# First block: 24 reciprocal square roots worked out on GpSimd instead of VectorE

## The chip, the cores and the metric

One core of a Trainium2 chip runs the whole program in one launch. The metric is the device time of an execution in microseconds (us). Engines are named as the profile names them: PE (TensorE matrix products; PEld are its weight loads), DVE (VectorE), ACT (ScalarE), POOL (GpSimd) and SP (SyncE, which issues the weight transfers). Each takes its instructions in a fixed order.

## The reference, cut to what matters

Two blocks follow each other. The first has two layers over 256 tokens `x` and 256 context tokens `xc`; the second has two layers of another kind (feed-forward, mixer, feed-forward). Only the first block's norms are touched.

```python
def _rmsnorm(x, g):
    y = xf * lax.rsqrt(jnp.mean(xf * xf, axis=-1, keepdims=True) + RMS_EPS)
    return y * g
def _layernorm(x, g, b):
    y = (xf - mu) * lax.rsqrt(var + LN_EPS)
    return y * g + b
...
def _layer(x, xc, ...):
    h = _rmsnorm(x, norm_g) * (1 + scale) + shift            # modulate()
    hp = h @ w_in
    q, k, v: _rmsnorm(hp[Q]) @ w_uq, _rmsnorm(hp[KV]) @ w_ukv  # mla()
    conv: silu(_layernorm(depthwise_conv31(glu))) @ w_pw      # conv_out()
    sgu:  u * (w_s @ _layernorm(v))                           # sgu()
    y = concat(attn, conv, fourier, sgu) * silu(hp[GATE])
    x = x + gate * (y @ w_out)
```

## The kernel before

Four tiles of 128 tokens (t = 0, 1 of `x`, t = 2, 3 of `xc`) go through the first layer together; in the second layer the context tiles only give keys and values. All of a layer's weights stream through as tiles of 512 KB: DMA (`raw`), ACT rounds them (`whi`), DVE takes the rest (`wlo`), and PE makes three products of each (`u` for the input projection, `yo` for the output projection). Beside this stream, Python generators give the side work of each branch: `mla` (queries, keys, values), `sgu`, `conv` (31 steps of `acc` on DVE) and `conv_out`, `fourier`, `attend`, and `ada_rest` (long dot products `adaj` on DVE, which make the modulation vectors of the next stages). `modulate` makes the second layer's input.

A planner in the kernel (`Sched`) keeps a clock for each engine. `S.dve`, `S.act` and `S.pool` add a planned cost and issue the instruction; a generator is resumed when the planned clock passes what it waits for. The framework's own list scheduler then settles each engine's final order from these instructions and their dependencies. So planned lengths decide who stands behind whom, on all engines, and on the chip each engine waits in that order.

The norms need 1/sqrt(w) for one or two numbers in each row. `rsqrt` does it by a bit trick (`rs_y` from the integer view of `w`, `rs_h` = -w/2) and three Newton steps, each instruction dependent on the one before. On DVE a step for one column is two instructions (`rs_t`, `rs_y`). There are 24 such chains in the first block: 12 in `layernorm` (six from `sgu`, six from `conv_out`; ten DVE instructions from `rwl` to `lnb`), 4 in `modulate` (nine), and 8 in `mla` (six with two columns, twelve instructions; two with one, nine). A `layernorm` chain's result goes to ACT (`ln`), for `sgu` then to two DVE instructions (`ln<-ln,rows`) and the PE product `sgum`; for `conv_out` to PE transposes (`tpc<-ident,ln`), ACT (`cs`) and the PE product `pw`. A `modulate` chain scales `xn`, which PE transposes (`tpx`) for the next layer's `u` and `kv`. An `mla` chain's result is the scale of ACT's copies `qkf` and `V`.

Before the change POOL only clears buffers (MEMSET of `qkf`, `qz`, `glu`) and issues a few transfers (`xc`, `final_g`, `grow`).

Of the kernel before, what the change touches and what calls it, by code (L numbers as in the profile page):

```python
# [19 lines left out]
EPS = 1e-6  # L20
# [73 lines left out]
LN_EPS = 1e-5  # L94
# [72 lines left out]
class Sched:  # L167
# [201 lines left out]

def rsqrt(S, ch, pool, w, n, tag):

    y = pool.tile([P, n], F32, tag=tag + "y", name="rs_y", bufs=4)
    h = pool.tile([P, n], F32, tag=tag + "h", name="rs_h")
    t = pool.tile([P, n], F32, tag=tag + "t", name="rs_t")
    S.dve(ch, n, "tensor_scalar", y.bitcast(I32), w.bitcast(I32), -0.5, float(0x5F3759DF), op0=ALU.mult, op1=ALU.add)
    S.dve(ch, n, "tensor_scalar", h, w, -0.5, None, op0=ALU.mult)
    for _ in range(3):
        if n == 1:  # L380
            S.dve(ch, n, "scalar_tensor_tensor", t, y, h, y, op0=ALU.mult, op1=ALU.mult, x=0.06)
        else:
            S.dve(ch, n, "tensor_tensor", t, y, y, op=ALU.mult)
            S.dve(ch, n, "tensor_tensor", t, t, h, op=ALU.mult)
        S.dve(ch, n, "scalar_tensor_tensor", y, t, 1.5, y, op0=ALU.add, op1=ALU.mult)
    return y


# [577 lines left out]
class First:  # L966
# [293 lines left out]
    def modulate(self, t, l, x, ch, ss, ev):  # L1260

        S, s = self.S, t // 2
        new = self.hp.tile if t < 2 else self.p1.tile
        kw = (dict(tag="hhi"), dict(tag="hlo")) if t < 2 else (dict(tag="s4", bufs=S4),) * 2
        hi, lo = (new([P, KT, P], F32R, name=n, **k) for n, k in zip(("hhi", "hlo"), kw))
        w = self.small.tile([P, 1], F32, tag="rw", name="rw")
        S.dve(ch, 1, "scalar_tensor_tensor", w, ss[:, 0:1], EPS, ss[:, 1:2], op0=ALU.add, op1=ALU.add)
        r = rsqrt(S, ch, self.small, w, 1, "r")
        xn = [self.normed(Chain(ch.t), x, r, n, n == 1) for n in range(2)]
        yield ch  # L1270
        for n in range(2):
# [12 lines left out]
            S.act(ch, 512, "copy", hi[:, h, :], f)
            S.dve(ch, 512, "tensor_sub", lo[:, h, :], f, hi[:, h, :].bitcast(F32))
            if n == 0:
                S.done(ev, ch)
        self.hs[t] = lambda k: (hi[:, k, :], lo[:, k, :])


    def layernorm(self, ch, src, n):

        S = self.S
        st = self.small.tile([P, 6], F32, tag="bn", name="bn")
        mv = self.small.tile([P, 2], F32, tag="mv", name="mv", bufs=4)
        S.dve(ch, n, "bn_stats", st, src)
        S.dve(ch, 6, "bn_aggr", mv, st)
        w = self.small.tile([P, 1], F32, tag="rw", name="rwl")
        S.dve(ch, 1, "tensor_scalar", w, mv[:, 1:2], LN_EPS, None, op0=ALU.add)
        r = rsqrt(S, ch, self.small, w, 1, "r")  # L1300
        b = self.small.tile([P, 1], F32, tag="lnb", name="lnb", bufs=4)
        S.dve(ch, 1, "scalar_tensor_tensor", b, mv[:, 0:1], -1.0, r, op0=ALU.mult, op1=ALU.mult)
        z = self.w2([P, 256], "ln")
        S.act(ch, 256, "activation", z, src, AF.Identity, scale=r, bias=b, x=0.15)
        return z
# [216 lines left out]
    def mla(self, t, ps, kv_only=False):  # L1522
        nc, S, l = self.nc, self.S, self.l[t]
        s, i = divmod(t, 2)
        o = 0 if kv_only else 256
        kv0 = 96 if kv_only else 256
        ch = S.chain()
        w = 160 if kv_only else 416
        p0 = 96 if kv_only else 0
        a = self.w2([P, 416], "mla")  # L1530
        S.act(ch, w, "copy", a[:, :w], ps[:, p0:p0 + w])
        ss = self.small.tile([P, 2], F32, tag="ssm", name="ssm", bufs=4)
        if not kv_only:

            jk = self.w2([P, 256], "jq")
            S.act(ch, 256, "activation", jk, a[:, :256], AF.Square, scale=math.sqrt(96.0 / 256), accum_out=ss[:, 0:1], x=0.09)
        jk = self.w2([P, 256], "jk")
        S.act(ch, 128, "activation", jk[:, :P], a[:, o:o + P], AF.Square, scale=math.sqrt(1.0 / 128), accum_out=ss[:, 1:2],
              x=0.09)
        if kv_only:  # L1540
            S.dve(ch, 1, "tensor_scalar", ss[:, 1:2], ss[:, 1:2], EPS, None, op0=ALU.add)
            r = rk = rsqrt(S, ch, self.small, ss[:, 1:2], 1, "r")
        else:
            S.dve(ch, 2, "tensor_tensor", ss, ss, self.eps2, op=ALU.add)
            r = rsqrt(S, ch, self.small, ss, 2, "r2")
# [24 lines left out]
        S.act(ck, 256, "mul", self.L[l].V[t], pv[:, :, 64:], rk, x=0.09)  # L1570
        kr = a[:, o + P:o + P + 32]
        if s == 0:
            self.rotate(ck, kv[:, :, 64:96], kr.unsqueeze(1).to_broadcast([P, 4, 32]), i)
        else:
            S.act(ck, 128, "copy", kv[:, :, 64:96], kr.unsqueeze(1).to_broadcast([P, 4, 32]))
        cq = None
        if not kv_only:
            qv = kf[:, :, 1, :]
            pq = self.psum("ps", "pq")
            cq = S.chain()  # L1580
            for c in range(2):
# [364 lines left out]
```

## Time and profile before

| what | value |
|---|---|
| median of 3 runs | 1449.67 us (1449.08 to 1450.29) |
| the profiled execution, its own time | 1447.77 us |
| its span in the profile | 1446.0 us (1.77 us lie around it) |
| PE busy | 1403.1 us (97%) |
| DVE busy | 1002.7 us (69%) |
| ACT busy | 765.8 us (53%) |
| POOL busy | 30.0 us (2%), 46 instructions |
| TensorE clock granted, mean | 0.996 |

The first block takes the first 430 us or so of the span. A busy PE is not PE at its peak, since records of products overlap; what PE waits for is read from the timeline's brackets. The shares over the whole span hide that DVE is busy for nearly all of some stretches of the first block.

### The profile page before, as it was taken

How to read it: one execution, taken by the hardware profiler on the slowest of the kernel's cores; microseconds unless marked ns; L12 is line 12 of the kernel's file. 1: busy time of each engine (PE TensorE's matmuls, PEld its weight loads, DVE VectorE, ACT ScalarE, POOL GpSimd, SP SyncE). 2: the span in 40 equal slices, each digit the busy share in tenths (PEclk: the TensorE clock that was granted, in tenths of full speed). 3: DMA queues.
4: the chain of work that ended last, by engine and by line, in shares of the span. 5: the costliest groups of instructions: out<-in, count | busy, mean ns of one | idle time of the engine just before them, and what ended most of it. 6: DMA issues, size and time to landing. Idle time of an engine off the chain costs nothing.

```text
span 1446.0 us, 19092 instructions
## 1 busy us (share of the span) xinstructions
PE 1403.1 (97%) x6766; PEld 1134.5 (78%) x6766; DVE 1002.7 (69%) x2175; ACT 765.8 (53%) x1348; POOL 30.0 (2%) x46
## 2 busy tenths in 40 slices
PE   7999997999999999999999999999999999999997
PEld 4778886777877888777878888788887778788886
DVE  4899978779787555587886555765555878865554
ACT  4465533576565444567655444554445676554442
POOL 1000000000000000000000000000000000000000
PEclk9999999999999999999999999999999999999999
DMA  8751455333456555653446566566566534466551
GB/s 304 238 172 59 128 192 162 123 124 121 159 189 209 186 188 188 190 186 121 139 139 204 189 180 186 173 193 187 188 189 189 182 125 134 143 200 186 185 186 58
DMA packets 69088, 245.64 MB, mean 170 GB/s; under 512 B 7841, under 2 KB 8097, under 8 KB 68865
## 3 DMA queue, kind: packets, MB, share of 16 engines
q1 hardware_dynamic: 66384, 235.11, 51.1%
q0 software_dynamic: 2176, 8.79, 1.8%
q8 instruction: 53, 0.87, 0.2%
q10 hardware_dynamic: 432, 0.53, 0.1%
q14 instruction: 43, 0.34, 0.1%
HBM read 243.35 MB, written 1.05 MB: 169 GB/s over the span
## 4 chain that ended last, share of the span: by engine, by line
PE 79%; DVE 11%; DMA 4%; ACT 3%; issue 2%; SPq 0%; DVEq 0%; ACTq 0%
PE u L230 37%; PE y L230 18%; PE m L230 9%; DMA raw<-in_wst_dram 3%; PE yo L230 3%; DVE adaj L221 2%; DVE wlo L221 2%; PE av L230 2%; PE tpg L234 2%; DVE acc L221 1%; ACT whi L216 1%; PE tpp L234 1%; DMA ada<-in_adan_dram 1%; PE sc L230 1%; ACT f L216 1%
## 5 line engine op out<-in xcount | busy, mean ns | idle before, releaser
L221 DVE TENSOR_TENSOR wlo<-raw,whi 128x1024 fp32r<-128x1024 f32 (+1 forms) x380 | 459.2, 1211 | 341.8 <-ACT whi L216 339.4
L216 ACT CAST whi<-raw 128x1024 fp32r<-128x1024 f32 (+1 forms) x380 | 395.3, 1042 | 386.7 <-PE u L230 228.5
L230 PE MATMUL u<-whi,h_hi 128*128 128x512 f32 x704 | 281.2, 400 | 1.1 <-ACT h_hi L216 1.1
L230 PE MATMUL u<-whi,h_lo 128*128 128x512 f32 x704 | 275.0, 391 | 0.6 <-DVE h_lo L221 0.6
L230 PE MATMUL u<-wlo,h_hi 128*128 128x512 f32 x704 | 275.5, 392 | 0.0
L230 PE MATMUL y<-whi,g 128*128 128x512 f32 x704 | 218.3, 390 | 0.5 <-ACT g L216 0.5
L230 PEld LDWEIGHTS y<-whi,g 128*128 128x128 f32 x704 | 132.0, 188 | 28.8 <-ACT g L216 0.8
L230 PEld LDWEIGHTS u<-wlo,h_hi 128*128 128x128 f32 x704 | 132.1, 188 | 27.7
L230 PEld LDWEIGHTS u<-whi,h_lo 128*128 128x128 f32 x704 | 132.5, 188 | 27.1 <-DVE h_lo L221 2.5
L230 PEld LDWEIGHTS u<-whi,h_hi 128*128 128x128 f32 x704 | 132.2, 188 | 26.4 <-ACT h_hi L216 1.7
L230 PE MATMUL y<-wlo,g 128*128 128x512 f32 x352 | 137.3, 390 | 0.0
L230 PE MATMUL u<-whi,hhi 128*128 128x512 f32 (+2 forms) x256 | 98.7, 388 | 0.4 <-ACT whi L216 0.3
L221 DVE CUSTOM_DVE_ANT_0 adaj<-ada,cbc 128x1024 bf16<-128x1024 f32 x76 | 90.6, 1221 | 8.7 <-DMA ada<-in_ada_dram 8.6
L230 PE MATMUL u<-wlo,hhi 128*128 128x512 f32 (+2 forms) x256 | 94.4, 372 | 0.4 <-DVE wlo L221 0.4
L230 PE MATMUL u<-whi,hlo 128*128 128x512 f32 (+2 forms) x256 | 94.8, 372 | 0.0
L230 PE MATMUL m<-whi,h_hi 128*128 128x512 f32 x192 | 79.0, 415 | 0.4 <-ACT h_hi L216 0.4
L230 PEld LDWEIGHTS y<-wlo,g 128*128 128x128 f32 x352 | 66.1, 188 | 14.3
L230 PE MATMUL m<-wlo,h_hi 128*128 128x512 f32 x192 | 75.5, 395 | 0.0
L230 PE MATMUL m<-whi,h_lo 128*128 128x512 f32 x192 | 75.3, 394 | 0.0
L221 DVE SCALAR_TENSOR_TENSOR acc<-glu,cw,acc 128x512 f32<-128x512 f32 (+1 forms) x120 | 70.8, 613 | 0.0
L230 PEld LDWEIGHTS u<-whi,hhi 128*128 128x128 f32 x256 | 48.2, 189 | 8.3 <-issue 1.9
L230 PEld LDWEIGHTS u<-wlo,hhi 128*128 128x128 f32 x256 | 48.2, 188 | 8.0 <-DVE wlo L221 1.2
(294 smaller groups left out, 1961.6 us busy)
## 6 DMA issues: line engine op xcount, KB each, us to landing
raw<-in_wst_dram SPq DMA_DIRECT2D x376, 512.0 KB, 3.6
ada<-in_ada_dram SPq DMA_DIRECT2D x42, 512.0 KB, 4.3
grow<-in_rows_dram POOLq DMA_DIRECT2D x10, 512.0 KB, 5.1
raw<-in_wst_dram SPq DMA_DIRECT2D x8, 416.0 KB, 3.1
ada<-in_adan_dram SPq DMA_DIRECT2D x6, 512.0 KB, 5.3
raw<-in_wst_dram SPq DMA_DIRECT2D x8, 256.0 KB, 2.8
tab<-in_tab_dram POOLq DMA_DIRECT2D x1, 1536.0 KB, 8.4
x<-in_x_dram SPq DMA_DIRECT2D x2, 512.0 KB, 5.4
```

Of the source, the lines that this page charges most:

```text
L216: ins = getattr(self.nc.scalar, fn)(*a, **k)
L221: ins = getattr(self.nc.vector, fn)(*a, **k)
L230: self.nc.tensor.matmul(*a, **k)
L234: self.nc.tensor.transpose(out, in_, ident)
```

## The change

The 24 chains run in POOL's queue. POOL has no instruction here that takes two operations and three operands, so `scalar_tensor_tensor` is split: a Newton step becomes four instructions, the chain of `layernorm` seventeen, that of `modulate` sixteen, each of `mla` fifteen. The planner counts 0.2 us for each (`tiny`), and 0.13 us from one to the next. The 4-column chain at the very start and those of the second block stay on DVE.

```diff
+    def tiny(self, ch, n, fn, *a, **k):
+
+        return self.pool(ch, 0.2, fn, *a, **k)
...
-def rsqrt(S, ch, pool, w, n, tag):
+def rsqrt(S, ch, pool, w, n, tag, small=None):
+    small = small or S.dve
...
-    S.dve(ch, n, "tensor_scalar", h, w, -0.5, None, op0=ALU.mult)
+    small(ch, n, "tensor_scalar", h, w, -0.5, None, op0=ALU.mult)
     for _ in range(3):
-        if n == 1:
-            S.dve(ch, n, "scalar_tensor_tensor", t, y, h, y, op0=ALU.mult, op1=ALU.mult, x=0.06)
+        if n == 1 and small == S.dve:
+            small(ch, n, "scalar_tensor_tensor", t, y, h, y, op0=ALU.mult, op1=ALU.mult, x=0.06)
         else:
-            S.dve(ch, n, "tensor_tensor", t, y, y, op=ALU.mult)
-            S.dve(ch, n, "tensor_tensor", t, t, h, op=ALU.mult)
-        S.dve(ch, n, "scalar_tensor_tensor", y, t, 1.5, y, op0=ALU.add, op1=ALU.mult)
+            small(ch, n, "tensor_tensor", t, y, y, op=ALU.mult)
+            small(ch, n, "tensor_tensor", t, t, h, op=ALU.mult)
+        if small == S.dve:
+            small(ch, n, "scalar_tensor_tensor", y, t, 1.5, y, op0=ALU.add, op1=ALU.mult)
+        else:
+            small(ch, n, "tensor_scalar", t, t, 1.5, None, op0=ALU.add)
+            small(ch, n, "tensor_tensor", y, t, y, op=ALU.mult)
...
-        S.dve(ch, 1, "tensor_scalar", w, mv[:, 1:2], LN_EPS, None, op0=ALU.add)
-        r = rsqrt(S, ch, self.small, w, 1, "r")
+        S.tiny(ch, 1, "tensor_scalar", w, mv[:, 1:2], LN_EPS, None, op0=ALU.add)
+        r = rsqrt(S, ch, self.small, w, 1, "r", S.tiny)
         b = self.small.tile([P, 1], F32, tag="lnb", name="lnb", bufs=4)
-        S.dve(ch, 1, "scalar_tensor_tensor", b, mv[:, 0:1], -1.0, r, op0=ALU.mult, op1=ALU.mult)
+        S.tiny(ch, 1, "tensor_tensor", b, mv[:, 0:1], r, op=ALU.mult)
+        S.tiny(ch, 1, "tensor_scalar", b, b, -1.0, None, op0=ALU.mult)
```

`modulate` and `mla` are edited in the same way. Since the planned lengths change, much of the first block's order changes on every engine; the second block's order on PE does not.

First place: DVE at the first `sgu` norm of layer 1. Before, from the end of the statistics (`mv`), the chain stands between the long instructions:

```order
L221 BN_AGGR mv<-bn 128x2
L221 SCALAR_TENSOR_TENSOR acc<-glu,cw_100,acc 128x512
L221 TENSOR_SCALAR rwl<-mv 128x1
L221 TENSOR_REDUCE mx_1100<-sc_1098 128x1
L221 TENSOR_SCALAR rs_y<-rwl 128x1
L221 TENSOR_SCALAR rs_h<-rwl 128x1
L221 TENSOR_REDUCE mx_1110<-sc_1107 128x1
L221 SCALAR_TENSOR_TENSOR rs_t<-rs_y,rs_h 128x1
L221 SCALAR_TENSOR_TENSOR acc<-glu,cw_100,acc 128x512
L221 SCALAR_TENSOR_TENSOR rs_y<-rs_t,rs_y 128x1
```

and DVE at the same place now:

```order
L221 BN_STATS bn<-u_879 128x6
L221 SCALAR_TENSOR_TENSOR acc<-glu,cw_100,acc 128x512
L221 BN_AGGR mv<-bn 128x2
L221 SCALAR_TENSOR_TENSOR acc<-glu,cw_100,acc 128x512 x4
L221 TENSOR_TENSOR ln<-ln,rows_112 128x256
L221 SCALAR_TENSOR_TENSOR acc<-glu,cw_100,acc 128x512
L221 TENSOR_TENSOR ln<-ln,rows_112 128x256
```

The chain has left DVE's queue; four `acc` stand between the statistics and `ln`, which needs the chain's result.

Second place: PE at the product `sgum` of that norm. Before (`dft` is the Fourier branch, `u` the projection of another tile):

```order
L230 MATMUL dft<-cnsn,F_1041 128x512 x2
L230 MATMUL u_1156<-whi_779,hhi 128x512
L230 MATMUL u_1156<-whi_779,hlo 128x512
L230 MATMUL u_1156<-wlo_780,hhi 128x512
...
L230 MATMUL dft<-cnsn,F_1041 128x512 x2
L230 MATMUL sgum<-ln,ws 128x64 x4
```

and PE there now:

```order
L234 MATMUL u_1192<-whi_795,hlo 128x512
L234 MATMUL u_1192<-wlo_796,hhi 128x512
L238 MATMUL tpp_1209<-ident,p_1133 128x128 x2
L234 MATMUL sgum<-ln,ws 128x64 x4
L234 MATMUL dft<-cnsn,F_1005 128x512 x2
```

The two `dft` pieces and the six `u` products between them stood ahead of `sgum`, and now stand behind it.

Third place: PE at the first `conv_out` of layer 1 (its transposes `tpc<-ident,acc`). Before it stands among the output projections `yo`:

```order
L234 MATMUL tpy<-ident,y_1271 128x128 x2
L230 MATMUL yo_2317<-wlo_2248,yT_2034 128x512
L230 MATMUL yo_2317<-whi_2247,yT_2034 128x512
L230 MATMUL yo_2317<-whi_2247,yT_2035 128x512
...
L230 MATMUL yo_2445<-whi_2247,yT_2035 128x512
L234 MATMUL tpc<-ident,acc 128x128 x2
```

and PE there now:

```order
L234 MATMUL u_1854<-wlo_1604,hhi 128x512
L234 MATMUL u_1854<-whi_1603,hhi 128x512
L238 MATMUL tpc<-ident,acc 128x128 x2
L234 MATMUL u_1854<-whi_1603,hlo 128x512
L238 MATMUL tpc<-ident,acc 128x128 x2
L234 MATMUL u_1854<-wlo_1604,hhi 128x512
```

`conv_out` of layer 1, its eight `pw` products included, now stands among the input projections, ahead of the first `yo`.

## Rows read from the trace of the kernel before

**Rows 1.** Stretches: length, busy PE, PEld, DVE, ACT, POOL, PE's clock, DMA, GB/s
```profile
97.00:217.00 120.00, 118.75 (x656) 99.99 (x656) 110.46 (x251) 56.98 (x130) 1.07 (x2) 1.00 0.40 128
...
246.00:256.00 10.00, 9.66 (x45) 7.60 (x44) 6.25 (x14) 4.13 (x12) 0.00 (x0) 0.85 0.40 132
```
**Rows 2.** PE's waits from 216 to 256 us: total, times, longest
```profile
PE tpc L234 <- ACT ln L216: 4.0, 1, 4.0
...
PE tpy L234 <- DVE y L221: 3.5, 1, 3.5
```
**Rows 3.** Timeline of DVE and ACT at the first sgu norm, and PE's sgum
```profile
100.92 0.18 DVE L221 BATCH_NORM_AGGREGATE mv<-bn 128x2 f32<-128x6 f32 x1
...
107.00 0.17 DVE L221 SCALAR_TENSOR_TENSOR lnb<-mv,rs_y 128x1 f32<-128x1 f32 x1
...
107.26 0.56 ACT L216 ACTIVATE ln<-u,lnb,rs_y 128x256 f32<-128x256 f32 x1 [1.76 <-DVE mv L221]
...
108.93 0.42 DVE L221 TENSOR_TENSOR ln<-ln,rows 128x256 f32<-128x256 f32 x1
...
106.29 1.88 PE L230 MATMUL dft<-cnsn,F 128*128 128x512 f32 x4
...
111.12 1.00 PE L230 MATMUL sgum<-ln,ws 128*128 128x64 f32 x8
```
**Rows 4.** Chain that ended last: one stretch of the projection on PE
```profile
189.28 9.32 PE u L230 x41
```
**Rows 5.** Groups on DVE from 0 to 430 us: busy, mean ns
```profile
L221 DVE CUSTOM_DVE_ANT_0 adaj<-ada,cbc 128x1024 bf16<-128x1024 f32 x76 | 90.6, 1221 | 8.7 <-DMA ada<-in_ada_dram 8.6
...
L221 DVE SCALAR_TENSOR_TENSOR acc<-glu,cw,acc 128x512 f32<-128x512 f32 x60 | 43.8, 744 | 0.0
...
L221 DVE SCALAR_TENSOR_TENSOR rs_y<-rs_t,rs_y 128x1 f32<-128x1 f32 x57 | 8.7, 156 | 0.4
```
**Rows 6.** Timeline of one modulate chain: its first instruction and its user
```profile
269.76 0.16 DVE L221 SCALAR_TENSOR_TENSOR rw<-ssx 128x1 f32<-128x1 f32 x1 [0.85 <-ACT junk L216]
...
271.55 0.49 DVE L221 TENSOR_SCALAR xn<-x,rs_y 128x512 f32<-128x512 f32 x1
```
**Rows 7.** Groups on POOL: one of the smallest MEMSETs
```profile
L1012 POOL MEMSET eps<- 128x1 f32 x1 | 0.1, 118 | 0.0
```
**Rows 8.** Timeline: a transfer on POOL, and what it waited for
```profile
208.90 0.68 DVE L221 TENSOR_TENSOR wlo<-raw,whi 128x512 fp32r<-128x512 f32 x1
...
209.78 0.54 POOL L1737 DMA_DIRECT2D xc<-in_ctx_dram  x1 [23.88 <-DVE wlo L221]
```
**Rows 9.** Timeline of two MEMSETs on POOL and a DVE instruction between them
```profile
285.53 0.97 POOL L226 MEMSET qkf<- 128x1024 f32 x1
...
285.62 1.18 DVE L221 TENSOR_SCALAR xn<-xc,rs_y 128x512 f32<-128x512 f32 x1
...
286.90 0.95 POOL L226 MEMSET qkf<- 128x1024 f32 x1 [0.40 <-issue]
```
**Rows 10.** Timeline: the four mla chains, first and last; uses of the last two
```profile
73.64 0.15 DVE L221 TENSOR_TENSOR ssm<-ssm,eps 128x2 f32<-128x2 f32 x1
...
83.44 0.15 DVE L221 SCALAR_TENSOR_TENSOR rs_y<-rs_t,rs_y 128x2 f32<-128x2 f32 x1
...
87.73 0.47 ACT L216 ACTIVATE qkf<-pkv,rs_y 128x256 f32<-128x256 f32 x1 [0.18 <-PE pkv L230]
...
95.02 0.47 ACT L216 ACTIVATE qkf<-pkv,rs_y 128x256 f32<-128x256 f32 x1 [0.28 <-PE pkv L230]
```
**Rows 11.** Timeline of PE at conv_out of layer 1: two pieces of pw
```profile
246.13 3.35 PE L230 MATMUL pw<-pw,cs 128*128 128x256 f32 x8
...
250.25 1.13 PE L230 MATMUL pw<-pw,cs 128*128 128x256 f32 x4 [0.33 <-ACT cs L216]
```
**Rows 12.** Timeline at the start of layer 2's projections
```profile
282.22 0.68 DVE L221 TENSOR_TENSOR hlo<-f,hhi 128x512 fp32r<-128x512 f32 x1
...
284.78 0.39 PE L230 MATMUL u<-whi,hhi 128*128 128x512 f32 x1
```

More of the change, by code (lines that the diff above doesn't have):

```diff
@@ L376, in rsqrt @@
     t = pool.tile([P, n], F32, tag=tag + "t", name="rs_t")
-    S.dve(ch, n, "tensor_scalar", y.bitcast(I32), w.bitcast(I32), -0.5, float(0x5F3759DF), op0=ALU.mult, op1=ALU.add)
-    S.dve(ch, n, "tensor_scalar", h, w, -0.5, None, op0=ALU.mult)
+    small(ch, n, "tensor_scalar", y.bitcast(I32), w.bitcast(I32), -0.5, float(0x5F3759DF), op0=ALU.mult, op1=ALU.add)
+    small(ch, n, "tensor_scalar", h, w, -0.5, None, op0=ALU.mult)
     for _ in range(3):
-        if n == 1:
-            S.dve(ch, n, "scalar_tensor_tensor", t, y, h, y, op0=ALU.mult, op1=ALU.mult, x=0.06)
-        else:
-            S.dve(ch, n, "tensor_tensor", t, y, y, op=ALU.mult)
-            S.dve(ch, n, "tensor_tensor", t, t, h, op=ALU.mult)
-        S.dve(ch, n, "scalar_tensor_tensor", y, t, 1.5, y, op0=ALU.add, op1=ALU.mult)
+        if n == 1 and small == S.dve:
+            small(ch, n, "scalar_tensor_tensor", t, y, h, y, op0=ALU.mult, op1=ALU.mult, x=0.06)
+        else:
+            small(ch, n, "tensor_tensor", t, y, y, op=ALU.mult)
[5 more added lines that the diff above has]
+            small(ch, n, "tensor_tensor", y, t, y, op=ALU.mult)
     return y
@@ L1266, in modulate @@
         w = self.small.tile([P, 1], F32, tag="rw", name="rw")
-        S.dve(ch, 1, "scalar_tensor_tensor", w, ss[:, 0:1], EPS, ss[:, 1:2], op0=ALU.add, op1=ALU.add)
-        r = rsqrt(S, ch, self.small, w, 1, "r")
+        S.tiny(ch, 1, "tensor_scalar", w, ss[:, 0:1], EPS, None, op0=ALU.add)
+        S.tiny(ch, 1, "tensor_tensor", w, w, ss[:, 1:2], op=ALU.add)
+        r = rsqrt(S, ch, self.small, w, 1, "r", S.tiny)
         xn = [self.normed(Chain(ch.t), x, r, n, n == 1) for n in range(2)]
@@ L1298, in layernorm @@
         w = self.small.tile([P, 1], F32, tag="rw", name="rwl")
-        S.dve(ch, 1, "tensor_scalar", w, mv[:, 1:2], LN_EPS, None, op0=ALU.add)
-        r = rsqrt(S, ch, self.small, w, 1, "r")
+        S.tiny(ch, 1, "tensor_scalar", w, mv[:, 1:2], LN_EPS, None, op0=ALU.add)
+        r = rsqrt(S, ch, self.small, w, 1, "r", S.tiny)
         b = self.small.tile([P, 1], F32, tag="lnb", name="lnb", bufs=4)
-        S.dve(ch, 1, "scalar_tensor_tensor", b, mv[:, 0:1], -1.0, r, op0=ALU.mult, op1=ALU.mult)
+        S.tiny(ch, 1, "tensor_tensor", b, mv[:, 0:1], r, op=ALU.mult)
+        S.tiny(ch, 1, "tensor_scalar", b, b, -1.0, None, op0=ALU.mult)
         z = self.w2([P, 256], "ln")
@@ L1540, in mla @@
         if kv_only:
-            S.dve(ch, 1, "tensor_scalar", ss[:, 1:2], ss[:, 1:2], EPS, None, op0=ALU.add)
-            r = rk = rsqrt(S, ch, self.small, ss[:, 1:2], 1, "r")
-        else:
-            S.dve(ch, 2, "tensor_tensor", ss, ss, self.eps2, op=ALU.add)
-            r = rsqrt(S, ch, self.small, ss, 2, "r2")
+            S.tiny(ch, 1, "tensor_scalar", ss[:, 1:2], ss[:, 1:2], EPS, None, op0=ALU.add)
+            r = rk = rsqrt(S, ch, self.small, ss[:, 1:2], 1, "r", S.tiny)
+        else:
+            S.tiny(ch, 2, "tensor_tensor", ss, ss, self.eps2, op=ALU.add)
+            r = rsqrt(S, ch, self.small, ss, 2, "r2", S.tiny)
             rk = r[:, 1:2]
```

## The prediction

> **What bounds the kernel now.** I read the page first: PE is busy 97% of the span, which says little of the first block, so I went by stretches. From 97 to 217 us PE is busy 118.75 of 120 us at full clock, and DVE 110.46 [rows 1]. PE sets the pace there (a product of the projection goes by in 9.32 / 41 = 0.23 us [rows 4]), and DVE keeps up only just. Then I asked for PE's waits. Between 216 and 256 us it stands idle twice: 3.5 us before a transpose of `y` that DVE made late, and 4.0 us before the transposes of `conv_out`, which wait for ACT's `ln` [rows 2]. That `ln` is the user of two of the chains that are now moved. Behind the second wait the granted clock is 0.85 over ten us [rows 1], and eight passes of `pw` take 3.35 us where four take 1.13 [rows 11]. Last I followed single chains through the timeline. The first `sgu` norm needs from the end of `mv` at 101.10 to the end of `lnb` at 107.17, 6.1 us, since a long instruction stands between any two of its own; its `ln` on ACT and the two on DVE end at 109.35, and PE comes to `sgum` only at 111.12 [rows 3]. So the chain is long there and costs PE nothing: 1.8 us are to spare. Where DVE has nothing else to do, the nine instructions of a `modulate` chain take 271.55 - 269.76 = 1.79 us, 0.20 us for each link [rows 6].
>
> **What the change removes.** 12 chains of ten, 4 of nine, 6 of twelve and 2 of nine are 246 instructions on DVE. Each is some 0.156 us long [rows 5], so they are 38 us of DVE's time at the very most. By itself that is worth nothing: PE runs without a gap where DVE is fullest [rows 1]. I cost it at 0; the most that I would grant is the 3.5 us by which `y` is late [rows 2].
>
> **What it adds.** 12 x 17 + 4 x 16 + 8 x 15 = 388 instructions on POOL, each of which waits for the one before. No row shows such an instruction. From below: POOL's smallest MEMSET takes 0.118 us [rows 7], with no read and no hand-over. From above: a link that has to wait for a whole long instruction on DVE, 0.74 us for `acc` and 1.22 us for `adaj` [rows 5]. Between them: a DVE instruction of this size takes 0.156 us [rows 5], and POOL starts its transfer at 209.78, 0.20 us after the `wlo` that it waited for ended at 209.58 [rows 8]. I add the two and take **0.35 us for a link**, nearer to the lower end, since in rows 6 and 7 small work takes tenths of a us and nothing in it waits for a stranger. A `layernorm` chain is then 17 x 0.35 = 5.95 us, one of `modulate` 5.6 us, one of `mla` 5.25 us. Against 6.1 us in the crowded stretch that is no gain, and against 1.79 us on an idle DVE it is three times as long.
>
> The Trainium skill (GPSIMD Engine Reference, Engine selection) says that elementwise work belongs on VectorE and that GpSimd is about twice as slow for operations with two inputs. Rows 6 against my estimate say the same for another reason, the number of links; no run here yet shows the speed itself.
>
> **Where it lies on the path**, place by place, at 0.35 us:
>
> - *sgu, layer 1.* The order now leaves four `acc` (3.0 us at 0.744 us each [rows 5]) between `mv` and `ln` on DVE, and has put `sgum` on PE in front of two `dft` pieces (1.88 us each [rows 3]) and six products (0.23 us each): PE reaches it 5.1 us earlier, at about 106.0. The data come at 101.10 + 5.95 + 2.2 (from `lnb` to the last `ln`, 109.35 - 107.17 [rows 3]) = 109.2. PE stands 3.2 us at the first; the other three have three or four such DVE instructions between `mv` and `ln` by the order, so the like. As some of it will overlap with waits already there, I take 2 us each: **+8** (bounds 0 and 4 x 3.2 = 13).
> - *conv_out, layer 1.* Its work moves from among the `yo` to before them, and some fifty products of the projection lie between its first transposes and the use of `ln`: 11 us of cover for a chain of 6 us. The 4.0 us wait and its neighbour of 0.3 us go, and with them the slow clock, 3.35 - 2 x 1.13 = 1.1 us on `pw` [rows 2, 11]: **-5.5** (bounds 0 and, with the 3.5 us wait above, -9).
> - *mla, layer 1.* The four chains stand in POOL's queue one behind the other. From 73.64 they end at 78.9, 84.1, 89.4 and 94.6; on DVE the last ended at 83.6. ACT uses the third at 87.73 and the fourth at 95.02 [rows 10]: **+2** for the third. Two MEMSETs of `qkf`, about 0.95 us each [rows 9], stand behind all four chains, but their buffers are wanted no earlier.
> - *modulate.* Tile 0's `hlo` ends at 282.90 and the next layer's `u` starts at 284.78 [rows 12], 1.9 us to spare, and the chain is 5.6 - 1.8 = 3.8 us longer: +1.9. The context tiles come later; I add 1: **+3** in all.
> - *layer 2.* Two `sgu` norms and four `mla` chains wait in the same way, but PE is less full there, and `conv_out` moves forward again: **+1** (bounds -3 and +6).
>
> The transfers on POOL (`xc`, `final_g`) now stand behind chains, but are wanted tens of us later: 0. Sum: 8 - 5.5 + 2 + 3 + 1 = **+8.5 us**, on the profiled execution's own 1447.77 us 1456.3. The median of the runs is 1.9 us above that execution, so I predict 1449.67 + 8.5 = **1458 us**, slower. A difference under 0.2% (2.9 us) I call no change; it is about what a measurement of this kernel can tell.
>
> **The rivals.**
>
> *Faster: POOL's link is as short as DVE's.* For it: 0.20 us is what a link costs in rows 6, and POOL's small MEMSET is no longer than DVE's small work. Against it: the 0.20 us after `wlo` in rows 8 is a hand-over alone. At 0.20 us a chain is 3.4 us, `sgum` has its data at 106.7, waits fall to about 0.4 us each (1.8 in all), `mla` and `modulate` are in time, and `conv_out` gives its 5.5: -3.7, or -7.2 if the late `y` goes as well. I put it at 1444 us. Between -3.7 at 0.20 us and +8.5 at 0.35 us the sum is zero near 0.245 us: that link length decides.
>
> *No change.* The same sum with a link of 0.21 to 0.28 us: what the earlier `conv_out` gives, the `sgum` waits take. About 1450 us.
>
> *Much slower: POOL waits for DVE.* When a MEMSET ran on POOL from 285.53 to 286.50, DVE's `xn` took 1.18 us where it takes 0.49 without one, and ended at 286.80; the next MEMSET, which waited for nothing that the profile shows, began only at 286.90 [rows 6, 9]. So the two engines can shut each other out for an instruction. If a POOL link has to wait for a long instruction with two inputs in SBUF, the four `mla` chains meet about twelve `adaj` and `wlo` (half of 1.22 us each, +7) and each `sgu` chain four `acc` (0.74 in place of 0.35 us, +6 over four): 8.5 + 13 = +21.5, 1471 us. Against it: rows 9 show a writer on POOL against a copy on DVE, not small reads against products. It can't run away, since DVE soon stands still on `ln` or `rot` and lets POOL through.
>
> The Trainium skill (SBUF — State Buffer, Who interferes with whom) names this rule: GpSimd shares a port pair with VectorE, held for a whole instruction, and a VectorE instruction with two SBUF inputs shuts out a GpSimd instruction that reads SBUF. By that the rival above is the rule; rows 9 agree on the exclusive hold, and no row shows the case of two inputs.
>
> **How the numbers follow.** Forecast 0.44; faster 0.24; no change 0.16; much slower 0.16. So faster 0.24, same 0.16, slower 0.60. The range takes in the lower half of the faster rival's span and the upper rival with some of its unknown: 1443 to 1476. The forecast's own range is 1453 to 1463.
>
> **What would show it.** In the changed profile: POOL's small instructions, start to start in one chain, at 0.30 to 0.40 us; PE waiting for `sgum` four times, 1 to 4 us each, with DVE idle before `ln`; no wait of `tpc` for `ln` between 216 and 256 us, and no stretch at a clock of 0.85 there; ACT's `qkf` waiting on POOL. The second block's length should not move. I am wrong if a link takes under 0.25 us, if the `sgum` waits are hidden, or if the new order of the transfers and `adaj`, which I cost at nothing, moves the path by more than the chains do.

## The result, and the profile after

The changed kernel takes 1522.74 us (median of 4 runs, 1522.49 to 1523.77) against 1449.38 us before: a ratio of 1.0508, 95% interval 1.0490 to 1.0527, 73 us slower. The forecast was slower by 8.5 us, with 1476 us as the upper end. The sign was right; the size was not.

All of it lies in the first block. The first product of the second block (`u<-whi,h_hi`) starts at 426.05 us before and at 501.05 us now, and from there to the end both take some 1020 us. The windows of the changed kernel (columns as in [rows 1]):

```profile
60.00:500.00 440.00, 370.62 (x1818) 299.77 (x1818) 290.64 (x568) 206.56 (x462) 117.98 (x399) 0.91 0.37 118
97.00:217.00 120.00, 101.66 (x493) 80.89 (x492) 88.29 (x174) 52.66 (x119) 33.70 (x116) 0.92 0.24 76
217.00:256.00 39.00, 35.88 (x200) 29.76 (x199) 27.79 (x59) 15.44 (x38) 5.17 (x32) 0.98 0.44 140
256.00:450.00 194.00, 149.37 (x693) 120.13 (x692) 111.99 (x213) 84.69 (x181) 57.35 (x199) 0.87 0.37 121
...
212.00:219.00 7.00, 4.72 (x14) 3.82 (x15) 1.13 (x4) 1.02 (x2) 4.13 (x26) 0.51 0.01 4
```

From 97 to 217 us PE was busy 118.75 of 120 us at full clock [rows 1]; now it is busy 101.66 at a mean granted clock of 0.92, and from 256 to 450 us 149 of 194 at 0.87, so that for a quarter of that time the lower of the two levels, 1.2 GHz, is granted (a mean of 0.87 between 1 and 0.5). Two losses stand beside each other. PE's waits of 0.25 us or more between 60 us and the end of the block add up to 68.9 us, where before they were 14.0: 55 of the 75 us. The other 20 us are time in which PE is busy: 372 us from 60 us to the end of the block, where before they were 351. Products are slower at the lower clock: one of `u<-whi,hhi` and its like goes by in 0.43 us there and in 0.23 us at full clock (medians of the changed kernel), and the lower clock is granted for 75 us of the block now, for 7 us before.

PE's waits in the changed kernel from 0 to 460 us (total, times, longest):

```profile
PE tpx L238 <- ACT f L216: 13.6, 3, 11.3
PE tpm L238 <- ACT T L216: 12.2, 1, 12.2
...
PE yo L234 <- DVE wlo L221: 6.1, 1, 6.1
PE tpp L238 <- ACT ln L216: 6.0, 2, 4.0
PE tpc L238 <- ACT ln L216: 5.4, 1, 5.4
PE pkv L234 <- ACT cT L216: 5.3, 2, 3.4
PE tph L238 <- POOL rs_y L230: 5.1, 1, 5.1
```

No `sgum` is among them, where I had looked for four waits, and only one line names POOL. PE waits mostly for ACT. The waits of ACT and DVE from 60 to 500 us say what those wait for in turn:

```profile
ACT ln L216 <- POOL lnb L230: 44.8, 10, 7.4
...
ACT qkf L216 <- POOL qkf L230: 16.6, 2, 9.3
...
ACT xn L216 <- POOL rs_y L230: 15.2, 4, 4.5
```
```profile
DVE ln L221 <- ACT ln L216: 32.4, 6, 10.0
DVE xn L221 <- POOL rs_y L230: 17.4, 4, 5.2
```

In these three rows ACT stands 76.6 us behind POOL; before, it stood 22.7 us behind DVE's chains for the same users.

The chains themselves. The timeline of POOL and DVE in the first mla chain:

```profile
74.10 0.20 POOL L230 TENSOR_TENSOR rs_t<-rs_y 128x2 f32<-128x2 f32 x1
74.23 1.22 DVE L221 CUSTOM_DVE_ANT_0 adaj<-ada,cbc 128x1024 bf16<-128x1024 f32 x1 [0.75 <-DMA ada<-in_ada_dram]
74.37 1.14 POOL L230 TENSOR_TENSOR rs_t<-rs_t,rs_h 128x2 f32<-128x2 f32 x1
...
75.39 1.22 DVE L221 CUSTOM_DVE_ANT_0 adaj<-ada,cbc 128x1024 bf16<-128x1024 f32 x1
75.60 1.10 POOL L230 TENSOR_SCALAR rs_t<-rs_t 128x2 f32<-128x2 f32 x1
...
76.78 0.20 POOL L230 TENSOR_TENSOR rs_y<-rs_t,rs_y 128x2 f32<-128x2 f32 x1
```

A link that is busy for 0.20 us lasts 1.14 us when it falls into an `adaj`, and ends 0.06 us after it. That is the "much slower" rival's mechanism, at its place. The Trainium skill (SBUF — State Buffer, Who interferes with whom) has it as a rule, that a VectorE instruction with two SBUF inputs shuts out a GpSimd instruction that reads SBUF; this trace agrees. Thirteen of the 60 links of the first four mla chains last over 1 us, and the chains take 31.2 us together (72.85 to 104.01), 0.52 us a link. Undisturbed, a link is 0.28 us from start to start.

The trace also gives the whole sum of these holds. Of the 388 links 68 last over 0.3 us; beside each stands a long instruction on DVE (39 times `acc`, 13 times `wlo`, 11 times `adaj`, five others). What the 68 take beyond 0.2 us adds up to 36.8 us, so a link is some 0.37 us long in the mean.

The first `sgu` norm (compare [rows 3]):

```profile
101.82 0.16 DVE L221 BATCH_NORM_AGGREGATE mv<-bn 128x2 f32<-128x6 f32 x1
101.92 2.69 DVE L221 SCALAR_TENSOR_TENSOR acc<-glu,cw,acc 128x512 f32<-128x512 f32 x4
...
103.95 1.84 POOL L230 MEMSET qkf<- 128x1024 f32 x2
104.93 0.47 ACT L216 ACTIVATE qkf<-pkv,rs_y 128x256 f32<-128x256 f32 x1 [7.24 <-POOL qkf L230]
...
105.87 0.23 POOL L230 TENSOR_SCALAR rwl<-mv 128x1 f32<-128x1 f32 x1
...
110.28 0.22 POOL L230 TENSOR_SCALAR lnb<-lnb 128x1 f32<-128x1 f32 x1
110.53 0.56 ACT L216 ACTIVATE ln<-u,lnb,rs_y 128x256 f32<-128x256 f32 x1 [1.25 <-POOL lnb L230]
111.13 0.43 DVE L221 TENSOR_TENSOR ln<-ln,rows 128x256 f32<-128x256 f32 x1 [6.52 <-ACT ln L216]
```

The chain is 4.6 us, shorter than the 6.1 us of before. But POOL is still at the mla chains and their MEMSETs, so it starts 3.9 us late; DVE, with its four `acc` done, stands 6.5 us; and ACT stands 7.2 us for a `qkf` whose MEMSET was queued behind the last `mla` chain.

The longest wait of PE, 12.2 us, comes about in the same way in layer 2. ACT stands 9.3 us for a `qkf` whose MEMSET is queued behind four `mla` chains. The statistics `mv` of the layer's first `sgu` norm end at 381.98 us, but its chain starts only behind that MEMSET, 7.3 us later, and ACT stands 3.8 us more at `ln`. ACT's `T`, which needs nothing of the `sgu` chain, stands behind both, and PE waits for `T`:

```profile
389.19 0.47 ACT L216 ACTIVATE qkf<-pkv,rs_y 128x256 f32<-128x256 f32 x1 [9.31 <-POOL qkf L230]
389.24 0.21 POOL L230 TENSOR_SCALAR rwl<-mv 128x1 f32<-128x1 f32 x1
...
393.86 0.56 ACT L216 ACTIVATE ln<-u,lnb,rs_y 128x256 f32<-128x256 f32 x1 [3.83 <-POOL lnb L230]
...
394.78 0.58 ACT L216 COPY T<-tph 128x512 f32<-128x512 f32 x1
...
395.42 0.48 PE L238 MATMUL tpm<-ident,mla 128*128 128x128 f32 x1 [12.23 <-ACT T L216]
```

### The profile page after: what moved, and what is told of

The parts are those of the page before. It is cut to its first block, busy times and chain, and to the rows that moved or that the text cites. A ratio compares the mean times of both kernels' runs of the same rounds, so it can differ in the third digit from the quotient of the medians.

```text
span 1522.0 us, 19271 instructions
## 1 busy us (share of the span) xinstructions
PE 1424.0 (94%) x6766; PEld 1148.8 (75%) x6766; DVE 982.1 (65%) x1929; ACT 767.0 (50%) x1348; POOL 139.8 (9%) x434
## 4 chain that ended last, share of the span: by engine, by line
PE 69%; issue 7%; DVE 6%; POOL 5%; ACT 2%; DMA 2%; DVEq 0%; POOLq 0%; ACTq 0%; SPq 0%
PE u L234 33%; PE y L234 17%; PE m L234 8%; POOL rs_t L230 3%; PE yo L234 2%; PE tpg L238 1%; DMA ada<-in_ada_dram 1%; POOL rs_y L230 1%; PE av L234 1%; DVE wlo L221 1%; DMA raw<-in_wst_dram 1%; PE tpp L238 1%; DVE x L221 1%; PE tpx L238 1%; PE cum L234 1%
## 5 line engine op out<-in xcount | busy, mean ns | idle before, releaser
L234 PEld LDWEIGHTS u<-wlo,h_hi 128*128 128x128 f32 x704 | 132.1, 188 | 27.7
L234 PE MATMUL u<-whi,hhi 128*128 128x512 f32 (+2 forms) x256 | 102.7, 403 | 2.5 <-ACT whi L216 2.2
L445 POOL DMA_DIRECT2D grow<-in_rows_dram x10 | 5.3, 531 | 654.8 <-DVE rw L221 637.7
```

The lines of the kernel that those rows point to most:

```text
L234: self.nc.tensor.matmul(*a, **k)
L445: self.nc.gpsimd.dma_start(g, self.rows[l, j:j + 1, :].to_broadcast([P, D]))
```

## The experiments

**Chains or order?** The planner's costs set most of the order. E1 and E2 cross the two: the one keeps the changed kernel's plan and runs the old chains on DVE, the other keeps the old plan and runs the chains on POOL.

```diff
 # E1, on the kernel before (links: how many of POOL's links an old instruction stands for)
+    def tiny(self, ch, n, fn, *a, x=0.0, links=1, **k):
+        for _ in range(links):
+            self.issue("pool", ch, 0.2)
+        return getattr(self.nc.vector, fn)(*a, **k)
...
 # E2, on the changed kernel (plan=False: the second half of a split instruction)
-        return self.pool(ch, 0.2, fn, *a, **k)
+        if plan:
+            self.issue("dve", ch, 0.07 + n * 0.00104 + x)
+        return getattr(self.nc.gpsimd, fn)(*a, **k)
```

E1 was expected to show:

> The planner counts as in the changed kernel (0.2 us for each of POOL's links), so that the order on PE, ACT and SP is nearly that of the changed kernel (95 of 5319 rows differ on PE, 41 of 1115 on ACT, none on SP); the chains themselves are the old instructions and run on VectorE. Theory A (the 73 us come from how long the chains take on POOL): within 15 us of the kernel before, 1435 to 1465 us. Theory B (they come from the new order, with its transfers and adaj in other places): most of the loss stays, 1500 to 1525 us.

E2 was expected to show:

> The mirror image: the planner counts as before the change (the chains on its VectorE clock), so that the order on SP and ACT is nearly that of before (2 of 464 and 69 of 1111 rows differ; 232 of 5315 on PE); the chains run as the split instructions on POOL. Theory A: the loss is there or larger, since nothing was planned around the longer chains: 1500 to 1560 us. Theory B: within 15 us of the kernel before, 1435 to 1465 us.

Measured: E1 1469.66 us, ratio 1.0137 (1.0122 to 1.0152); E2 1522.16 us, 1.0499 (1.0483 to 1.0515). The chains on POOL cost 72 us in an order that knows nothing of them. The new order, with the old chains on a DVE that the plan takes to be free of them, costs 20 us, which I had put at 0; that is 5 us above theory A's range and far below theory B's. They don't add up: with both changes, it is 73. So theory A holds in the main, and the order's own price is small beside it. One place where the order costs by itself is a transfer: in the changed kernel an `adaj` waits 4.42 us for its `ada` on DVE, with two `wlo` queued behind it, and PE's `yo` stands 6.06 us:

```profile
291.28 1.23 DVE L221 CUSTOM_DVE_ANT_0 adaj<-ada,cbc 128x1024 bf16<-128x1024 f32 x1 [4.42 <-DMA ada<-in_ada_dram]
...
294.98 2.35 DVE L221 TENSOR_TENSOR wlo<-raw,whi 128x1024 fp32r<-128x1024 f32 x2
...
296.25 0.79 PE L234 MATMUL yo<-wlo,yT 128*128 128x512 f32 x1 [6.06 <-DVE wlo L221]
```

E1 has the same wait of PE, 3.9 us long. PE's waits in E1 are 15 us longer in all than before; what the larger ones there wait for (`pkv` for ACT's `cT`, 6.3 us, and `tpx` for ACT's `f`, 5.4 us) stays open.

E3 changes one number (`self.pool(ch, 0.5, ...)` for 0.2). E4 leaves out two of three Newton steps on POOL, with their plan kept:

```diff
-    for _ in range(3):
+    for k in range(3):
+        if k and small != S.dve:
+            for _ in range(4):
+                S.issue("pool", ch, 0.2)
+            continue
```

E3 was expected to show:

> The changed kernel with one number changed: the planner counts 0.5 in place of 0.2 us for each of POOL's small operations, so a link is 0.63 us in the plan where the trace shows 0.28 us undisturbed and 0.36 us in the mean. Theory A, if the plan puts users too early: the users come later in the order and the waits shrink, 1460 to 1495 us. Theory A, if lateness can't be planned away because each engine's queue is fixed: about 1520 us. Theory B has no say on the direction, but the time would move by tens of us either way.

E4 was expected to show:

> Two of the three Newton steps are left out of the chains on POOL (a layernorm chain has 9 links in place of 17); the planner still counts them, so the order is that of the changed kernel but for 32 of 5319 rows on PE and 15 on ACT. Theory A: each chain is 8 links shorter, 2.2 us at 0.28 us and up to 5 us where VectorE's long instructions hold POOL up; with a wait at about a dozen places and the slower clock behind each, 30 to 50 us come back: 1470 to 1495 us. Theory B: no change, 1515 to 1525 us.

Measured: E3 1533.69 us, 1.0582 (1.0565 to 1.0600); E4 1483.78 us, 1.0236 (1.0215 to 1.0258). Planning a longer chain does not cure it; the time rises by 11 us, which neither branch of the expectation foretold. 192 links fewer in nearly the same order bring 39 us back, 0.2 us for each, as theory A had it.

**Which site?** The old plan, with the chains of one site alone on POOL (the others as before the change; PE's order differs from before in 40 to 198 of 6766 instructions of the trace, ACT's in 4 to 39 of 1348):

```diff
+SITES = ("sgu",)        # E6 "conv_out", E7 "mla", E8 "modulate"
...
+        small = S.tiny if site in SITES else S.dve
```

E5 was expected to show:

> Planned as before the change; only the six sgu chains run on POOL, the other 18 on VectorE as before. Theory A1 (the chains hurt each other: those of sgu start late since POOL is still at the mla chains and its MEMSETs, 105.87 in the changed kernel where the statistics ended at 101.98): alone they hurt little, a chain is 17 x 0.28 = 4.8 us where before it took 6.1 us, 1448 to 1456 us. Theory A2 (each chain costs by its own links): 6 of 24 chains, 102 of 388 links, so some 19 of the 72 us, 1464 to 1474 us.

E6 was expected to show:

> Planned as before; only the six conv_out chains run on POOL. Theory A1: two chains come at once there, and take 7.8 us interleaved in the changed kernel, a few us more than on VectorE, at up to three places on the path: 1452 to 1464 us. Theory A2: some 19 us, 1464 to 1474 us. If the four us that PE waited before (tpc for ln) were owed to long instructions between the links on VectorE, it gets faster by up to 3 us instead.

E7 was expected to show:

> Planned as before; only the eight mla chains run on POOL. In the changed kernel the first four of them ran one behind the other from 72.85 to 104.0 us, where on VectorE they took 73.64 to 83.6, and 12 of their 60 links took over 1 us beside a long instruction on VectorE. Theory A1: this is the largest part, with PE waiting for tph in layer 1 and tpm or pkv in layer 2: 1470 to 1490 us. Theory A2: 120 of 388 links, some 22 us, 1468 to 1476 us.

E8 was expected to show:

> Planned as before; only the four modulate chains run on POOL. Each takes 16 x 0.28 = 4.5 us and more, where before it took 1.8; at least two of them lie on the path at the start of layer 2, with the slower clock behind: 1454 to 1464 us by both theories. If they are hidden by other tiles' products, 1449 to 1452 us.

| site | chains | us | ratio (95%) | lost |
|---|---|---|---|---|
| E5 `sgu` | 6 | 1476.88 | 1.0191 (1.0176 to 1.0207) | 27.7 |
| E6 `conv_out` | 6 | 1462.83 | 1.0094 (1.0079 to 1.0109) | 13.6 |
| E7 `mla` | 8 | 1468.51 | 1.0130 (1.0114 to 1.0146) | 19.3 |
| E8 `modulate` | 4 | 1464.57 | 1.0105 (1.0087 to 1.0122) | 15.4 |

The sum is 76.0 us, E2 has 72: each site pays for itself. That goes against A1 (chains that hurt each other). By links alone (A2) it does not come out either: `sgu`, with 102 of the 388 links, costs most, 27.7 us where A2 had 15 to 25, and `conv_out`, with as many links, half of that.

E6 and E8 also say what the hold is worth. Reckoned as above, it adds 5.7 us to E6's chains and 3.4 us to E8's, 6 links in each, and these two lose 13.6 and 15.4 us all the same. From their last statistics on, the first two `modulate` chains of E8 have no link over 0.3 us, and DVE stands 5.3 and 5.2 us for them.

**By which way does a late chain reach PE?** ACT before the change at the first `sgu` norm (`ln` follows at 107.26 [rows 3]), and E5 at the same place:

```profile
105.13 0.37 ACT L216 COPY F<-u 128x256 f32<-128x256 f32 x1 [5.94 <-PE u L230]
```
```profile
100.28 0.17 DVE L224 BATCH_NORM_AGGREGATE mv<-bn 128x2 f32<-128x6 f32 x1
...
106.63 0.21 POOL L230 TENSOR_SCALAR lnb<-lnb 128x1 f32<-128x1 f32 x1
106.88 0.56 ACT L219 ACTIVATE ln<-u,lnb,rs_y 128x256 f32<-128x256 f32 x1 [8.33 <-POOL lnb L230]
107.47 0.42 DVE L224 TENSOR_TENSOR ln<-ln,rows 128x256 f32<-128x256 f32 x1 [3.47 <-ACT ln L219]
...
109.88 0.37 ACT L219 COPY F<-u 128x256 f32<-128x256 f32 x1
...
110.30 2.08 PE L238 MATMUL dft<-cnsn,F 128*128 128x512 f32 x2 [3.64 <-ACT F L219]
```

From the end of `mv` to the end of `lnb` are 6.4 us, about as long as before (6.1 us). What changed is who waits. Before, DVE did `acc` between the links, and ACT copied `F` ahead of `ln`. Now `ln` stands ahead of `F` in ACT's queue, ACT stands 8.3 us, DVE 3.5 us, and PE waits 3.6 us for `F`, which needs nothing of the chain. Over E5's six norms ACT stands 37.0 us and DVE 25.1 us; before, DVE never stood there, and ACT 18.3 us. Five experiments on E5 each work on one part of this:

```diff
 # E9: both ln of DVE to POOL
-        S.dve(ch, 256, "tensor_tensor", z, z, rows[:, :256], op=ALU.mult)
...
+            S.issue("dve", ch, 0.07 + 256 * 0.00104)
+            self.nc.gpsimd.tensor_tensor(z, z, r, op=op)
 # E13: four of ACT's ln behind a copy that was issued later
+        for i, j in LATER:
+            tc.add_manual_dep(S.acts[i], S.acts[j].name,
                              mybir.DependencyInfo(mybir.DependencyClass.NoSync, mybir.DependencyReason.DATA), reason="later")
 # E14: ln on DVE in place of ACT
-        S.act(ch, 256, "activation", z, src, AF.Identity, scale=r, bias=b, x=0.15)
...
+            self.nc.vector.tensor_scalar(z, src, r, b, op0=ALU.mult, op1=ALU.add)
 # E17: E14, and each ln on DVE behind a later instruction, as in E13
 # E18: E5 with one Newton step in place of three, as in E4
```

E9 was expected to show:

> The sgu-only kernel with one thing more: the two 128x256 instructions `ln` behind ACT's `ln` run on POOL as well, with the plan untouched, so that VectorE no longer stands in its queue before a result of the chain (PE's, ACT's and SP's orders are those of the sgu-only kernel, row for row). Theory C (in the sgu-only kernel it is VectorE's four standstills of 3.5 to 4.5 us before `ln`, 16.6 us in a stretch where it is nearly full, that cost the 28 us): most comes back, 1450 to 1460 us. Theory D (it is PE's wait for the chain's result at sgum): the result comes no earlier, and the time stays at 1472 to 1485 us.

E13 was expected to show:

> The sgu-only kernel with four of ACT's six `ln` moved one to ten places back in ACT's queue, behind copies that do not need the chain (F, whi, T, qkf); the orders on PE and VectorE differ in 25 and 30 rows, those on POOL and SP not at all. Theory F (a chain's user stands too early in ACT's fixed queue, and ACT, standing for 5 to 8 us each time, holds up F, p, T and pT, for which PE then waits): the 3.6 us at dft for F go, and part of the 4.8 us at tph, with the clock behind them: 1462 to 1472 us. Theory A2 (each link costs, wherever its user stands): 1474 to 1480 us.

E14 was expected to show:

> The sgu-only kernel with the six `ln` of sgu, u x r + b, on VectorE in place of ACT, the plan untouched: ACT never stands for these chains, VectorE still does, and has 6 instructions more (20 of PE's rows differ, none of POOL's and SP's). Theory F (ACT's standing, 37 us over six times in the sgu-only kernel, is what costs): 12 to 25 of the 28 us come back, 1452 to 1465 us. Theory C (VectorE's standing): 1472 to 1485 us. With the ninth experiment this is the second half of a pair: there VectorE was spared and ACT not.

E17 was expected to show:

> The fourteenth kernel (only sgu's chains on POOL, `ln` on VectorE) with one thing more: on VectorE each of the six `ln` is put two to five instructions back, behind `acc`, `mx` or `wlo` that do not need the chain; PE's order follows (75 rows; the second sgum stands 10 rows later, near its place before the change), POOL's and SP's not at all. Theory G (the order has the chain's users stand as if the chain were some 3 us long, where it takes 6.4; whichever engine's fixed queue holds the user stands still): most of what is left of the 22 us comes back, 1450 to 1461 us. Theory A2 (the links cost wherever the users stand): 1467 to 1475 us.

E18 was expected to show:

> The sgu-only kernel with two of the three Newton steps of its six chains left out (9 links in place of 17); nearly all of the order stays (7 rows differ on PE, 4 on ACT). A chain is then some 2.6 to 3.8 us. Theory G: that is about the room that the order leaves (3 to 4 acc of 0.74 us), so nearly nothing is lost any more: 1448 to 1456 us. Theory A2, in proportion to the links: 27.7 x 9 / 17 = 14.7 us stay, 1461 to 1467 us.

| kernel | us | ratio (95%) | lost |
|---|---|---|---|
| E5 | 1476.88 | 1.0191 (1.0176 to 1.0207) | 27.7 |
| E9, DVE spared | 1484.26 | 1.0248 (1.0231 to 1.0264) | 35.4 |
| E13, ACT's `ln` later | 1477.02 | 1.0202 (1.0182 to 1.0222) | 28.2 |
| E14, ACT spared | 1470.89 | 1.0159 (1.0142 to 1.0176) | 22.1 |
| E17, ACT spared, users later | 1463.03 | 1.0085 (1.0066 to 1.0104) | 13.2 |
| E18, 9 links | 1458.63 | 1.0061 (1.0044 to 1.0078) | 8.8 |

Theory C (DVE's standing) falls with E9: DVE no longer stands at `ln`, and the time rises. Theory D had the time right, but not the cause: in E5 PE waits for `sgum` once, 3.2 us of 30.4 us. E9's timeline says why it gains nothing:

```profile
102.88 4.05 DVE L224 SCALAR_TENSOR_TENSOR acc<-glu,cw,acc 128x512 f32<-128x512 f32 x6
102.92 0.75 POOL L230 TENSOR_TENSOR rs_t<-rs_t,rs_h 128x1 f32<-128x1 f32 x1
...
108.98 0.56 ACT L219 ACTIVATE ln<-u,lnb,rs_y 128x256 f32<-128x256 f32 x1 [9.49 <-POOL lnb L230]
...
111.45 0.16 DVE L224 RECIPROCAL rd<-den 128x1 f32<-128x1 f32 x1 [4.52 <-ACT p L219]
...
112.41 2.08 PE L238 MATMUL dft<-cnsn,F 128*128 128x512 f32 x2 [4.80 <-ACT F L219]
```

DVE runs on with six `acc`, each with two inputs in SBUF, and holds six links up to 0.56 to 0.75 us. The chain is 7.5 us in place of 6.4, ACT stands 9.5 us, and DVE then stands after all, for ACT's `p`.

E13 takes the wait for `F` away, and one of 3.8 us comes at the next Fourier product; ACT stands 22 us for the six norms, 15 us less than in E5, and the time is the same. E14 spares ACT (it no longer waits for `lnb`, but 34.8 us for DVE's `mx`, behind DVE's 22.4 us of standing) and gains 6 us, half of what theory F had at the least; theory F, ACT alone, falls too.

E17 puts the users where there is work to do meanwhile. It halves DVE's standing to 10.2 us and the loss of E5 to 13 us. That is most of theory G, but not all: the time lies between the two forecasts, for now the chains are longer, as in E9 (the first: 101.87 to 110.22, 8.4 us).

E18 leaves the order alone; its chains are 3.3 to 4.3 us. Two thirds of the loss are gone, more than the 47% of the links that were left out. It too lies between the forecasts, 2 to 3 us from either. ACT still stands 21.3 us and DVE 12.3 us there. Since E18 has nearly E5's order and loses 8.8 us, E5's own changes of order can hardly cost more than that.

So neither engine alone is the cause. What fits all of these is the gap between the chain's length (6 us and more) and the work that the order puts between it and its user (some 3 us), on whichever fixed queue the user stands; and work put into the gap on DVE lengthens the chain. E17 and E18 show both halves of this in direction; that it is the whole of the loss is not shown.

**POOL's queue.** E7 in layer 2. POOL runs four chains and then the four MEMSETs of `qkf`:

```profile
320.13 0.38 POOL L230 TENSOR_TENSOR ssm<-ssm,eps 128x2 f32<-128x2 f32 x1 [103.50 <-ACT jk L219]
...
340.37 3.65 POOL L234 MEMSET qkf<- 128x1024 f32 x4
...
341.38 0.47 ACT L219 ACTIVATE qkf<-pkv,rs_y 128x256 f32<-128x256 f32 x1 [12.26 <-POOL qkf L234]
...
342.28 0.79 PE L238 MATMUL u<-w,hhi 128*128 128x512 f32 x1 [6.80 <-ACT V L219]
```

ACT stands 12.3 us at the first `qkf`, not for its chain but for its MEMSET. E10 moves the MEMSETs to DVE (`self.nc.vector.memset(kf, 0.0)`); E12 is the changed kernel with this and with E9's edit.

E10 was expected to show:

> The mla-only kernel with the eight MEMSETs of qkf on VectorE in place of POOL, the plan untouched. Theory E (POOL's fixed queue: in the mla-only kernel ACT stood 12.3 us and 5.1 us at the first qkf of two tiles, whose MEMSET stood behind the chains of other tiles): 8 to 15 of the 19 us come back, 1454 to 1461 us. Theory A2 (the links' own length): within 4 us of the mla-only kernel, 1465 to 1472 us.

E12 was expected to show:

> The changed kernel with both remedies: `ln` of sgu on POOL, MEMSETs of qkf on VectorE; the plan, SP's order and nearly all of PE's (38 of 5319 rows differ) are those of the changed kernel. If theories C and E name the costs of sgu and mla, 25 to 45 of the 73 us come back: 1478 to 1498 us; what stays are the new order (20 us in the first experiment) and the chains of conv_out and modulate. If the links' length alone decides, 1515 to 1530 us.

Measured: E10 1463.39 us, 1.0100 (1.0085 to 1.0115): 5 of 19 us come back, and DVE has 7.3 us of MEMSETs more; between E and A2. ACT's waits for a MEMSET, 18.3 us over three times in E7, are gone, but it now waits 7.9 us for the chains themselves at the same `qkf` (1.7 us in E7). E12 1530.06 us, 1.0562 (1.0544 to 1.0581): worse than the change itself, as E9 would have it.

**Other versions.** E11 puts only `sgu`'s two `ln` on POOL in the kernel before; E15 puts all twelve `ln` of the norms on DVE there, E16 in the changed kernel (edits as E9 and E14).

E11 was expected to show:

> The kernel before the change, all chains on VectorE, with only the two 128x256 instructions `ln` of each sgu norm on POOL, the plan untouched: POOL gets 12 instructions with nothing behind them, and VectorE is spared 5 us of work and no wait is added to its queue. If VectorE's load sets the late `y` (3.5 us), 1 to 4 us faster, 1445 to 1449 us; if PE sets the pace there, no change, 1448 to 1451 us; if POOL's two instructions are held up beside VectorE's long ones and sgum comes late, 1452 to 1460 us.

E15 was expected to show:

> The kernel before the change with all twelve `ln` of the layernorms on VectorE, behind their chains on the same engine, the plan untouched. ACT stood 16.5 us over five times before `ln` there. If theory F holds there too, and VectorE has the room for 12 x 0.4 us: faster, 1440 to 1447 us. If VectorE is too full between 97 and 217 us, or ACT's standing was hidden there: 1448 to 1456 us.

E16 was expected to show:

> The changed kernel with all twelve `ln` on VectorE, the plan untouched (24 of PE's rows differ, 17 of ACT's). Theory F: ACT no longer stands 44.8 us over ten times for lnb; what stays are the mla and modulate chains and the new order: 1475 to 1498 us. Theory A2: 1515 to 1530 us.

Measured: E11 1458.59 us, 1.0071 (1.0054 to 1.0088), with PE waiting 6.3 us for `sgum` behind POOL's `ln`; E15 1448.24 us, 0.9995 (0.9986 to 1.0004), no change; E16 1514.07 us, 1.0454 (1.0438 to 1.0469), 9 of 73 us back. No version beat the kernel before. Groups on POOL in E9:

```profile
L1477 POOL TENSOR_TENSOR ln<-ln,rows 128x256 f32<-128x256 f32 x12 | 8.7, 725 | 3.9 <-ACT ln L219 3.4
```

An `ln` takes 0.725 us there and 0.42 on DVE [rows 3], 1.7 times as long. The Trainium skill (GPSIMD Engine Reference, Engine selection) says about twice for operations with two inputs; the trace roughly agrees.

## Why the prediction was wrong, step by step

- **The link, 0.35 us: about right in the mean, for a reason that I had only as a rival.** A link is 0.28 us undisturbed (0.27 in the first `sgu` chain), under the band of 0.30 to 0.40 us that I had named. The holds make it 0.37 in E5's first chain, 0.52 in the first four mla chains and some 0.37 in the mean. The link is not what failed: by my own sum 0.28 us gives +3 us and 0.37 us some +10.
- **"So the chain is long there and costs PE nothing", and then four waits at `sgum` of 2 us, +8: the step that failed.** I followed the chain to its own product. I did not ask what stands behind its user on ACT and DVE. `sgum` hardly waits; `F`, `dftz`, `pT` and `T`, which ACT makes behind `ln`, do. E5 has 27.7 us for the six norms. Its PE's waits are 16.4 us longer (30.4 us against 14.0), and the rest, 11.3 us, is a busier PE, 362 us against 351, with 34 us at the lower clock. In the sum of the forecast no term added a clock loss to a new wait; the only one was for a wait that I took away.
- **conv_out, -5.5, because some fifty products would cover the chain: wrong.** In the changed kernel PE goes through the first two tiles' transposes at 204.59 and 205.05 and then has fifteen products of `u`; the next `tpc` waits 5.4 us for ACT's `ln`, which reads the earlier transposes. Two chains run interleaved there, 206.06 to 214.07 us. E6, in the old place, lost 13.6 us. The slow stretch behind the old wait did go (0.98 from 217 to 256 us), but a new one stands around the new wait (0.51 from 212 to 219 us), and from 256 us on the clock is 0.87.
- **mla, +2, and the MEMSETs' "buffers are wanted no earlier": wrong.** E7 lost 19.3 us, 6 of it in layer 1; the MEMSETs are 5 us of the 19 by E10. In the changed kernel the four chains end at 104.0 us, not 94.6.
- **modulate, +3:** the mechanism was right, the size was not. E8 lost 15.4 us. From the last statistics on, a chain takes 4.3 us for the first two tiles and 5.4 to 5.5 us for the other two, where before it took 1.8; PE's waits for `tpx` behind ACT's `f` grow from 1.4 to 8.5 us, and the clock from 300 to 350 us is 0.93.
- **layer 2, +1 with bounds of -3 and +6: wrong by the most.** In the changed kernel the first `u` product of layer 2 starts 47.5 us later than before (332.3 against 284.8 us), and the second block 75.0 us later, so 27.5 us are lost between (some of it by `modulate`). Of the single sites that the term covers, `sgu` loses 11 us there (E5), `conv_out` 6 (E6) and `mla` 12 (E7). My reason, that PE is less full there, does not hold: before the change PE was busy for 164 of the 170 us from 256 to 426 us.
- **The 246 instructions taken off DVE, 0:** nothing in the runs shows a gain from them.
- **The new order of the transfers and `adaj`, 0: not right either.** The whole new order, of which they are a part, costs 20 us when the chains stay on DVE (E1); beside the late chains it is not seen (E2 against the change). How much of the 20 us the transfers make was not separated.
- **"Much slower", 1471 us:** the exclusive hold is there as described, and its size in the chains is 36.8 us, over 68 links. What it costs in the kernel's time was not separated, but E6 and E8 lose their 13.6 and 15.4 us nearly without it. It is a part of the loss and not the whole.
- **The second block's length: right.**

What stays open: how the 72 us divide between the holds and the undisturbed links, and why the order's 20 us vanish beside the chains. No run tried `scalar_tensor_tensor` on POOL, so that it has to be split there is taken from the change and not shown.

## What to carry to other kernels

When a small chain moves to an idle engine, list what stands behind its *user* on every in-order engine, and compare the chain's whole length with the work that the order leaves in between. The first `sgu` chain cost PE nothing in DVE's full queue, which did other work between its links; on POOL it was about as long, and its users' queues stood still. Price a new wait on PE with the clock behind it (here 55 us of waits brought 20 us more). Whoever fills the gap should look whether the filling work and the chain shut each other out.

## What the runs showed of the hardware that I had not expected

Two dependent chains interleaved on POOL cost far less than two in turn: 34 links take 6.1 us (216.45 to 222.53 in the changed kernel), where 17 undisturbed ones take 4.6. A link is 0.28 us from start to start in a chain, and 0.15 us lie between instructions of different chains where they alternate:

```profile
210.69 0.19 POOL L230 TENSOR_TENSOR rs_t<-rs_y 128x1 f32<-128x1 f32 x1
210.84 0.18 POOL L230 TENSOR_TENSOR rs_y<-rs_t,rs_y 128x1 f32<-128x1 f32 x1
210.98 0.18 POOL L230 TENSOR_TENSOR rs_t<-rs_t,rs_h 128x1 f32<-128x1 f32 x1
```

So some 0.13 of 0.28 us is spent waiting for the link's own result (an estimate from these two spacings). The hold on POOL lasts to the end of DVE's instruction, and DVE pays nothing: `adaj` takes 1.219 us on average now and took 1.221 before [rows 5]. Beside `mx`, a reduction from PSUM (E5, 101.01 to 102.02 us), POOL's links took 0.19 and 0.22 us.
